# A backbone layer on one core: GLU of three token blocks moved beside the readout, its result kept on chip

## The chip, the core and the metric

The kernel runs on one core of a Trainium2 chip. The metric is the device time of one execution in microseconds, the median of several runs. The engines are PE (TensorE, matmuls), DVE (VectorE), ACT (ScalarE) and POOL (GpSimd); SP (SyncE) issues all loads and stores. Each engine works through its own instructions in order and waits at semaphores for the others. PE's granted clock is given as a share: 1.0 is 2.4 GHz, 0.5 is 1.2 GHz, and a mean between them says how long it ran at which.

## What is computed

One layer over 2048 latent tokens of 1024 channels with a prefix of 256 context tokens. Half of the channels go through RWKV-7 time mixing (a recurrence in both directions), half through a bidirectional S5 state space model; its output y ends in a gated linear unit (GLU):

```python
    z = jax.nn.gelu(y)
    out = z * jax.nn.sigmoid(z @ glu_w.astype(f32) + glu_b.astype(f32))
...
        x = x + mod_x[2] * (jnp.concatenate([rwkv_x, s5_x], axis=-1) @ w_out[layer])
        x = x + mod_x[5] * swiglu(modulate(rmsnorm(x, norm2_g[layer]), mod_x[3], mod_x[4]),
                                  ffn_w1[layer], ffn_w3[layer], ffn_w2[layer])
...
    return rmsnorm(x, final_g)
```

GLU, RWKV readout, output projection and FFN act on each token by itself.

## The kernel before

Tokens are worked through in four blocks of 512, in the tail from block 3 down to block 0, since the backward RWKV direction delivers the last tokens first. All matmuls are float32, written as a high and a low part: `split` (L1140) makes the high part on ACT (L1141) and the low part on DVE (L1142), and a product takes three matmuls, high by high, high by low and low by high.

A scheduler orders the instructions: the code's order is their priority, and an instruction of lower priority goes first where it can start earlier in the scheduler's own timing of the program. On the chip the resulting order of each engine is fixed.

The class `Tail` does what follows the mixers. `glu(b, put)` loads z of a block (L1171; into buffers of the tag s, in the tail ns), splits it, then for each of four groups m of 128 channels: loads and splits 128 columns of weights (wr, wh, wl), loads z again for the gate (L1183, tag t), does 12 matmuls of 512 columns (L1187), tanh (L1189), an affine step (L1190), and the product with z on POOL (L1192). `put` takes the result: `keep` splits it into the tiles H and L, from which the output projection reads; `store` writes it to the DRAM scratch `cat`, and `load` fetches it from there and then keeps it. `readout(b, put)` does the same for the RWKV half, in 8 steps of 128 channels by 256 tokens (first matmul L1207 or L1211, sums L1252, transposition L1257). `outproj` and the second part of `ffn` are one function, `product` (L1293 to L1295, 256 columns each); the first part of `ffn` is L1369 with 512 columns. `norm` makes the FFN's input.

Before the tail proper, `hybrid_block` runs block 3's GLU and output projection together with the last 12 units of the backward RWKV direction (`R.unit`, 128 tokens each: a triangular inverse, mostly on POOL, L1012 and L1019 on PE, then the chain of states L1045, L1050, L1059, L1072, L1074; the result YW is stored by L1083). The GLU of blocks 2, 1 and 0 stands there as well, between the steps of block 3's readout, and stores to `cat`. `ffn(3)` follows with lower priority. When the units are done, the pool f2 takes over the memory of the RWKV pool, and `T.aside` gives GLU and readout their buffers there, from which the steps for the next block run beside the FFN of the one before (`early`).

Of the kernel before, what the change touches and what calls it, by code (L numbers as in the profile page):

```python
# ---- part 1: adaLN vectors, norm1, input projection, conv; one block of tokens after the other
# [8 lines left out]
F32 = mybir.dt.float32  # L10
# [12 lines left out]
AHEAD = 3000     # priority of what feeds the tensor engine  # L23
# [12 lines left out]
ORDER4 = [t for t in ORDER if t[0] == "u"] + [t for t in ORDER if t[0] != "u"]       # of the last block  # L36
PLANE = {"r": 0, "k": 1, "kk": 2, "v": 3}       # of rkvk
CONV = {"r": 0, "k": 1, "v": 2}                 # of the conv's channels
# [28 lines left out]
def rsqrt(nc, y, t, x, out=None, spread=lambda a: a):  # L67
    """out = spread(1 / sqrt(x)), x positive: from the halved exponent, three steps of Newton; y, t: scratch"""
    stt = nc.vector.scalar_tensor_tensor
    nc.vector.tensor_scalar(y.bitcast(I32), x.bitcast(I32), -0.5, float(0x5f3759df), op0=OP.mult, op1=OP.add)  # L70
    for i in range(3):
        stt(t, x, -0.5, y, op0=OP.mult, op1=OP.mult)
        nc.vector.tensor_tensor(t, t, y, op=OP.mult)
        if i < 2 or out is None:
            stt(y, t, 1.5, y, op0=OP.add, op1=OP.mult)
        else:
            stt(out, spread(t), 1.5, spread(y), op0=OP.add, op1=OP.mult)
# [6 lines left out]
def mod_group(tc, I, K, S, wt, st, fp, n, tag="f"):  # L84
    """128 columns of the adaLN product; wt(), st(): tiles of 1024 and 256 words, fp: tag f"""
    nc = tc.nc
    sec, part = divmod(n, 8)
    mw = I["mod_w"][0].rearrange("(k p) c -> p k c", p=P)
    pm = fp.tile([P, 512], F32, name=tag, bufs=2 if tag == "pa" else None)
    w = wt().rearrange("p (k c) -> p k c", k=8)  # L90
    for kh in range(2):
        nc.sync.dma_start(w[:, 4 * kh:4 * kh + 4], mw[:, 4 * kh:4 * kh + 4, n * P:(n + 1) * P])
        for kc in range(4):
            nc.tensor.matmul(pm[32 * kc:32 * kc + 32, 0:P], K["scp"][:, 4 * kh + kc, :], w[:, 4 * kh + kc, :],
                             start=kh == 0, stop=kh == 1)
    st = st()
    rows = st[:, 0:P]
    nc.scalar.activation(rows, pm[:, 0:P], AF.Copy)
    pc = fp.tile([P, 512], F32, name="f")
    if sec in (2, 5):  # L100
        nc.tensor.matmul(pc[0:2, 0:P], K["sel"], rows, start=True, stop=True)
        mb = st[0:1, P:2 * P]
        nc.sync.dma_start(mb, I["mod_b"][:, n * P:(n + 1) * P])
        nc.vector.tensor_add(mb, pc[0:1, 0:P], mb)
        nc.sync.dma_start(S["gate"][sec // 3:sec // 3 + 1, part * P:part * P + P], mb)
    else:
        nc.tensor.matmul(pc[:, 0:2], rows, K["sel"], start=True, stop=True)
        o = VOFF["mod_b"] + n
        nc.vector.tensor_scalar(K["mcol"][:, sec, part, :], pc[:, 0:2], K["vec"][:, o:o + 1], None, op0=OP.add)


def mod_vectors(tc, K, sec, dst, g, j):
    """scale (1 + s) g and shift of one normalisation"""
# [6 lines left out]
class Front:  # L120
    """S: rkvk [4,512,NT], vt [2,NT,512], lora [128,NT], sg [96,NX], u [512,16,144], zh [12,128,3,64], gate [2,1024]"""

    def __init__(self, tc, I, K, S, p, p2, fp):
# [20 lines left out]
        # selectors of one head's row among 8  # L144
# [81 lines left out]
    def conv(self, bi, kind, q, pa):  # L226
        """-> (tile, tokens) with the conv's output for the tokens that this block completes"""
# [31 lines left out]
    def span(self, bi):  # L259
        """tokens that the conv completes with this block"""  # L260
        return ((0, 256), (256, 384), (640, 512), (1152, 512), (1664, 640))[bi]
# [37 lines left out]
    def block(self, bi, aside=iter(()), order=ORDER, wait=0):  # L299
        """aside: work to interleave, one piece after each tile but the first ones (wait)"""  # L300
# [64 lines left out]
# ---- part 2: S5  # L365
# [7 lines left out]
def acc_exp(nc, pool, x, shape, name):  # L373
    """exp(x) to float32's accuracy on DVE; x is overwritten."""
# [90 lines left out]
NTAB = 394      # per pair of groups: L1 68, L2 68, BR 64, BI 64, BS 64, CR 32, CI 32, RHO 2  # L465
# [3 lines left out]
def s5_setup(tc, I, K, S, sp, pp):  # L469
    """Tables of every pair of groups -> S: s5t [16,128,NTAB], s5p [16,128,2,2,144], s5d [64,16,16]"""  # L470
# [33 lines left out]
    # q = (lb - 1) / lam  # L504
# [18 lines left out]
    # mag^16 and phase^16, each twice along the free axis  # L523
# [18 lines left out]
    # to states on partitions: (re, im), then (-im, re)  # L542
# [25 lines left out]
    # B and C  # L568
# [32 lines left out]
    # D on the diagonal of the lag 0 block: rows (g even: 0..15, g odd: 48..63)  # L601
# [14 lines left out]
    # phase tables exp(i phi n), n = 0..143  # L616
# [26 lines left out]
def s5_pair(tc, gp, S, K, DD, g1, g2, ps):  # L643
    """One pair of groups. S: u, s5t, s5p, wd -> z"""
# [39 lines left out]
    # lag blocks  # L684
# [21 lines left out]
    # input -> state  # L706
# [61 lines left out]
def s5_pairs(tc, S, K, DD, gps, sets, ps):  # L768
    """the pairs gps, in the buffers of the sets in turn"""
    for gp in gps:  # L770
        g1, g2 = sets[gp % len(sets)]
        yield from s5_pair(tc, gp, S, K, DD, g1, g2, ps)
        yield


# ---- part 3: RWKV-7 in chunks of 64 tokens, one direction after the other

S05 = math.exp(-0.5)
NU = 18         # units of 128 tokens
# [3 lines left out]
class Rwkv:  # L783
    """S: rkvk, vt, lora -> y [2,512,NX] (per direction), pb [2,512,NX] (r * kd per direction).
    What belongs to the backward direction is reversed within each 128 tokens; only the rows that k and v give to
    BK, BT, AR and V stay in natural order."""

    def __init__(self, tc, I, K, S, pool, pw, ph, nq=2, nb=4):
# [8 lines left out]
        # causal masks; in the backward direction the rows of k and v are in natural order  # L797
        self.MS = r.tile([P, 2, 64], F32, name="MS")        # direction
        self.MI = r.tile([P, 2, 2, 64], F32, name="MI")     # direction, par
# [12 lines left out]
        self.hv = hv = r.tile([P, 8], F32, name="hv")   # ka/2 (4), 1-ka/2 (4)  # L812
# [3 lines left out]
        # low-rank factors in parts, rows (high, high, low) and the bias (high, low) on the inputs' (high, low, high), 1, 1  # L816
        self.W2A = r.tile([98, 2, 512], F32R, name="W2A")
        self.LT = r.tile([98, 2, 256], F32R, name="LT")
        self.back = r.tile([P, 4, 64], F32, name="back")        # the backward direction's state after the context
        nc.vector.tensor_copy(self.LT[96:98], ones[96:98, None, 0:1].to_broadcast([2, 2, 256]))  # L820
        self.SG = r.tile([P, 2, 4, 2, 65], F32, name="SG")      # two units
        nc.gpsimd.memset(self.SG, 0.0)
        self.use(r)
        # unit matrices, lane 8 e + b of 32 holds the columns 4 m + e of matrix b
# [13 lines left out]
    def use(self, pool):  # L838
        """what the units keep, in a pool of its own"""
# [8 lines left out]
    def base(self, h):  # L848
        """first natural token of unit h"""
# [32 lines left out]
    def lora(self, h):  # L882
        """units h and h + 1: tanh of half the low-rank products"""
# [98 lines left out]
    def inverse(self, h, dve):  # L982
# [18 lines left out]
        T2 = r.tile([P, 8, 4, 8], F32, name="T2")     # m, e, b  # L1001
# [94 lines left out]
# ---- part 4: RWKV readout, output projection, FFN, final norm, 512 tokens at a time  # L1096
# [10 lines left out]
class Tail:  # L1107
    """S: y, pb, rkvk (v), sg, z, gate -> out"""
# [18 lines left out]
    def aside(self, f2, fq):  # L1127
        """the parts before the FFN of the next blocks take their buffers here"""
        self.side = (f2, fq, "nt", "ns", "zh", "zl")
        nc = self.nc  # L1130
        self.ER = f2.tile([P, 2, P], F32R, name="ER")       # Cm and blk, both exact
# [12 lines left out]
    def parts(self, b, pool=None):  # L1144
        """the mixer's output as (high, low)"""
# [7 lines left out]
    def store(self, b, k, ts, x):  # L1153
        t0 = 512 * b
        self.nc.sync.dma_start(self.S["cat"][k * P:(k + 1) * P, t0 + ts.start:t0 + ts.stop], x)

    def load(self, b, ks):
        for k in ks:
            x = self.side[0].tile([P, 512], F32, name=self.side[3], bufs=2)
            self.nc.sync.dma_start(x, self.S["cat"][k * P:(k + 1) * P, 512 * b:512 * b + 512])  # L1160
            self.keep(b, k, slice(0, 512), x)

    def glu(self, b, put):
        """z sigmoid(z W + b), z = [channels, token mod 16, token / 16]"""
# [4 lines left out]
        for k in range(4):  # L1169
            z = f2.tile([P, 512], F32, name=tag_s, bufs=2)  # L1170
            nc.sync.dma_start(z.rearrange("p (s j) -> p s j", s=16), zd[k])  # L1171
            zh = f2.tile([P, 512], F32R, name=tag_h, bufs=5)
            zl = f2.tile([P, 512], F32R, name=tag_l, bufs=5)
# [23 lines left out]
    def readout(self, b, put):  # L1197
# [6 lines left out]
        def product(o, w, exact, x, scale=None):  # L1204
            """w^T (scale x), with aside in parts; exact: w has no low part"""
# [18 lines left out]
        for hf in range(2):  # L1224
# [7 lines left out]
            for hp in range(4):  # L1232
# [16 lines left out]
                # the variances with the tokens on the partitions, spread out by the transposition  # L1249
# [21 lines left out]
    def product(self, b, A, n, wsrc, grow, last):  # L1271
        """X1 += gate * (A^T W), A = list of (hi, lo) of [128, 512 tokens], wsrc(k, columns) in DRAM;
        last: with X1 done, its squares are summed up"""
# [107 lines left out]
    def final(self, b):  # L1381
# [8 lines left out]
        for j in range(4):  # L1390
# [8 lines left out]
           "s5t": (16, P, NTAB), "s5p": (16, P, 2, 2, 144), "s5d": (64, 16, 16), "y": (2, 512, NX), "pb": (2, 512, NX),  # L1399
           "cat": (D, NX)}  # L1400
# [7 lines left out]
def hybrid_block(tc, I, out):  # L1408
    with tc.tile_pool(name="dram", bufs=1, space=bass.MemoryType.DRAM) as dp, \
# [50 lines left out]
        with tc.tile_pool(name="f1", bufs=1, side="right") as f1, tc.tile_pool(name="fp", bufs=3, space=PSUM, side="right") as fp:  # L1460
# [5 lines left out]
            rest = chain(*[T.glu(b, T.store) for b in (2, 1, 0)])  # L1466
            for i, _ in enumerate(T.readout(3, T.keep)):
                for _ in range(1 + i % 2):
                    next(rest, None)
            run(rest)  # L1470
# [6 lines left out]
            with tc.tile_pool(name="f2", bufs=1) as f2, tc.tile_pool(name="fq", bufs=3, space=PSUM) as fq:  # L1477
                T.aside(f2, fq)
                for b in (3, 2, 1):
# [3 lines left out]
                    T.load(b - 1, range(4, 8))  # L1483
                    early = T.ffn(b, SPLITS[3:5])
                    for _ in T.readout(b - 1, T.keep):
# [29 lines left out]
```

## Time and profile before

| | |
|---|---|
| median of 3 runs | 3823.46 us (3818.53 to 3835.97) |
| span of the profiled execution, first to last instruction | 3809.6 us |
| median less that span | 13.9 us |
| PE busy | 3423.6 us, 90% |
| mean granted clock | 0.906 |

The span is that of one execution taken by the hardware profiler; the runs' times hold what lies around it as well. "Busy" is the time in which an engine works on an instruction, overlaps counted once in the rows by stretch.

### The profile page before, as it was taken

Reading aid. Unit: us, or ns where it says so; the run is one execution under the profiler, and the core shown is the slowest. Engines: PE = TensorE matmul, PEld = TensorE weight load, DVE = VectorE, ACT = ScalarE, POOL = GpSimd, SP = SyncE. Lnnn points to the kernel's source line nnn. Section 1 sums busy time; section 2 is a strip of 40 time slices with the busy share of each in tenths; the row PEclk is TensorE's granted clock in tenths of the full one; section 3 lists DMA queues with packets and bytes.
Section 4 is the critical chain, followed back from the end, with each engine's and each line's share of the span. In section 5 each row is a group of like instructions: output and inputs, shape, how many; then the busy total and the mean of one; then the engine's idle time right before and its main releaser. Section 6 shows DMA issues by size and latency. Waiting matters only on the chain. (4 is left out here: it accounts for less than half of the span.)

```text
span 3809.6 us, 70313 instructions
## 1 busy us (share of the span) xinstructions
PE 3423.6 (90%) x25311; PEld 2858.0 (75%) x25311; DVE 2480.0 (65%) x4726; ACT 1723.1 (45%) x3785; POOL 1840.0 (48%) x3184
## 2 busy tenths in 40 slices
PE   5698988988777898888889999999999999999998
PEld 3676666666556676677677888988889888998887
DVE  7768777776778978856666647476444854454444
ACT  3565656554434443444455544354333433343333
POOL 3456667567667766766776543223212321231212
PEclk9898989898757876777899999999999999999999
DMA  6654545454233453365623335354333533333333
GB/s 184 195 138 114 150 110 140 131 139 118 76 97 108 136 141 106 95 160 128 147 85 94 97 109 158 106 165 129 103 98 103 173 102 100 106 100 121 103 99 96
DMA packets 789020, 462.34 MB, mean 121 GB/s; under 512 B 182544, under 2 KB 766868, under 8 KB 788672
## 3 DMA queue, kind: packets, MB, share of 16 engines
q1 hardware_dynamic: 788672, 457.85, 42.6%
q8 instruction: 200, 3.28, 0.4%
q14 instruction: 148, 1.21, 0.1%
HBM read 382.34 MB, written 75.36 MB: 120 GB/s over the span
## 5 line engine op out<-in xcount | busy, mean ns | idle before, releaser
L1301 POOL TENSOR_TENSOR X<-X,t 128x256 f32<-128x256 f32 x464 | 380.1, 848 | 940.6 <-DVE t L1298 937.5
L997 POOL TENSOR_TENSOR tmp<-AT,T 128x60 f32<-128x60 f32 (+24 forms) x992 | 402.8, 406 | 252.5 <-DVE AT L990 134.5
L1142 DVE TENSOR_TENSOR wl<-wr,wh 128x512 fp32r<-128x512 f32 x368 | 263.4, 717 | 327.7 <-PE f L1369 280.1
L999 POOL TENSOR_TENSOR T<-T,tmp 128x60 f32<-128x60 f32 (+24 forms) x992 | 423.6, 427 | 64.3
L1141 ACT ACTIVATE wh<-wr 128x512 fp32r<-128x512 f32 x368 | 231.9, 631 | 453.0 <-PE f L1369 394.8
L1142 DVE TENSOR_TENSOR vl<-vr,vh 128x256 fp32r<-128x256 f32 x480 | 256.2, 535 | 265.2 <-ACT vh L1141 264.7
L1294 PE MATMUL f<-vl,gh 128*128 128x256 f32 x1408 | 396.4, 288 | 6.6 <-DVE vl L1142 6.4
L1369 PE MATMUL f<-H,wh 128*128 128x512 f32 x1408 | 389.6, 397 | 9.6 <-ACT s L1372 5.2
L1295 PE MATMUL f<-vh,gl 128*128 128x256 f32 x1408 | 389.4, 284 | 0.0
L1369 PE MATMUL f<-L,wh 128*128 128x512 f32 x1408 | 389.1, 395 | 0.0
L1141 ACT ACTIVATE vh<-vr 128x256 fp32r<-128x256 f32 x480 | 199.3, 416 | 418.4 <-PE f L1295 367.7
L1369 PE MATMUL f<-H,wl 128*128 128x512 f32 x1408 | 385.6, 395 | 1.0 <-DVE wl L1142 1.0
L1293 PE MATMUL f<-vh,gh 128*128 128x256 f32 x1408 | 370.0, 287 | 2.7 <-ACT vh L1141 2.1
L255 DVE SCALAR_TENSOR_TENSOR acc<-zb,cw,acc 128x512 f32<-128x512 f32 (+2 forms) x384 | 314.1, 833 | 46.9 <-ACT acc L251 36.1
L1369 PEld LDWEIGHTS f<-L,wh 128*128 128x128 f32 x1408 | 264.0, 189 | 59.5 <-issue 0.2
L1369 PEld LDWEIGHTS f<-H,wl 128*128 128x128 f32 x1408 | 262.1, 188 | 59.7 <-DVE wl L1142 1.8
L1369 PEld LDWEIGHTS f<-H,wh 128*128 128x128 f32 x1408 | 258.0, 189 | 64.0 <-ACT s L1372 5.8
L1294 PEld LDWEIGHTS f<-vl,gh 128*128 128x128 f32 x1408 | 269.0, 191 | 16.9 <-DVE vl L1142 10.3
L1295 PEld LDWEIGHTS f<-vh,gl 128*128 128x128 f32 x1408 | 269.2, 191 | 1.4
L1293 PEld LDWEIGHTS f<-vh,gh 128*128 128x128 f32 x1408 | 255.4, 191 | 10.8 <-ACT vh L1141 3.6
L222 PE MATMUL pa<-HI,wl 128*128 128x512 f32 (+1 forms) x712 | 210.2, 415 | 49.6 <-POOL wl L219 39.0
L222 PE MATMUL pa<-HI,wh 128*128 128x512 f32 (+1 forms) x712 | 215.7, 424 | 26.6 <-ACT wh L218 14.0
(458 smaller groups left out, 7602.6 us busy)
## 6 DMA issues: line engine op xcount, KB each, us to landing
wr<-in_ffn_w_dram SPq DMA_DIRECT2D x352, 256.0 KB
raw<-in_w_in_dram SPq DMA_DIRECT2D x178, 256.0 KB
vr<-in_ffn_w_dram SPq DMA_DIRECT2D x352, 128.0 KB
ld<-s_rkvk SPq DMA_DIRECT2D x36, 768.0 KB
mraw<-in_mod_w_dram SPq DMA_DIRECT2D x64, 256.0 KB
vr<-in_w_out_dram SPq DMA_DIRECT2D x128, 128.0 KB
gq<-s_gate SPq DMA_DIRECT2D x116, 128.0 KB
SV<-s_vt SPq DMA_DIRECT2D x144, 64.0 KB
```

The costliest lines, as they stand in the source:

```text
L222: nc.tensor.matmul(pa[:, :nt], w[:, kc, :], h[:, 4 * kh + kc, :nt], start=kh + i + kc == 0, stop=kh == 1 and i == 2 and kc == 3)
L255: nc.vector.scalar_tensor_tensor(ag, zb[:, i0 - 1 + a:i0 - 1 + a + nr, e:e + 64], tap(a, e), ag, op0=OP.mult, op1=OP.add)
L997: eng.tensor_tensor(tv, AT[:, l + 1:, l:l + 1].to_broadcast([P, n, m]), T[:, l:l + 1, 0:m].to_broadcast([P, n, m]), op=OP.mult)
L999: eng.tensor_tensor(T[:, l + 1:, 0:m], T[:, l + 1:, 0:m], tv, op=OP.add)
L1141: self.nc.scalar.activation(hi, x, AF.Copy)
L1142: self.nc.vector.tensor_tensor(lo, x, hi.bitcast(F32), op=OP.subtract)
L1293: mm(o, ah[:, js], vh, start=k == 0 and j % 2 == 0, stop=False)
L1294: mm(o, ah[:, js], vl, start=False, stop=False)
L1295: mm(o, al[:, js], vh, start=False, stop=k == n - 1 and j % 2 == 1)
L1301: nc.gpsimd.tensor_tensor(x, x, t[:, j], op=OP.add)
L1369: mm(p, a[:, kc, :], h[:, 4 * kh + kc, :], start=kh + i + kc == 0, stop=kh == 1 and i == 2 and kc == 3)
```

## The change

The GLU of blocks 2, 1 and 0 is no longer worked out during block 3's readout. Each is worked out in the tail, ahead of the readout of the same block in the same interleaving with `early`, and keeps its result in H and L at once. The scratch `cat`, its 12 stores and 12 loads and the functions for them go. The tail's pool f2 gets four buffers each for the parts of z, zh and zl. The text also loses its comments, and its line numbers from 1153 on are 9 to 15 lower.

```diff
-    def store(self, b, k, ts, x):
-        t0 = 512 * b
-        self.nc.sync.dma_start(self.S["cat"][k * P:(k + 1) * P, t0 + ts.start:t0 + ts.stop], x)
-
-    def load(self, b, ks):
-        for k in ks:
-            x = self.side[0].tile([P, 512], F32, name=self.side[3], bufs=2)
-            self.nc.sync.dma_start(x, self.S["cat"][k * P:(k + 1) * P, 512 * b:512 * b + 512])
-            self.keep(b, k, slice(0, 512), x)
-
     def glu(self, b, put):
...
-            zh = f2.tile([P, 512], F32R, name=tag_h, bufs=5)
-            zl = f2.tile([P, 512], F32R, name=tag_l, bufs=5)
+            nb = 5 if f2 is f1 else 4
+            zh = f2.tile([P, 512], F32R, name=tag_h, bufs=nb)
+            zl = f2.tile([P, 512], F32R, name=tag_l, bufs=nb)
...
             T.parts(3)
             run(T.glu(3, T.keep))
             T.outproj(3, range(4, 8))
-            rest = chain(*[T.glu(b, T.store) for b in (2, 1, 0)])
-            for i, _ in enumerate(T.readout(3, T.keep)):
-                for _ in range(1 + i % 2):
-                    next(rest, None)
-            run(rest)
+            run(T.readout(3, T.keep))
             T.outproj(3, range(4))
...
                     T.parts(b - 1, f1 if b == 2 else f2)
-                    T.load(b - 1, range(4, 8))
                     early = T.ffn(b, SPLITS[3:5])
-                    for _ in T.readout(b - 1, T.keep):
+                    for _ in chain(T.glu(b - 1, T.keep), T.readout(b - 1, T.keep)):
                         next(early, None)
                     run(early)
```

On PE, amid the readout of block 3, the order before has GLU matmuls (f<-gh,wh and its kind) between readout (L1207, L1252) and RWKV (L963):

```order
L1187 MATMUL f<-gh,wh 128x512
L1187 MATMUL f<-gl,wh 128x512
L1187 MATMUL f<-gh,wl 128x512
L1207 MATMUL f<-yl,Cm 128x256
L963 MATMUL w<-Q,BK 128x128 x8
L1207 MATMUL f<-pl,RK 128x256
L1207 MATMUL f<-sg,g_17011 128x256
L1252 MATMUL f<-blk,yl 128x2 x2
```

The changed order at the same place has readout (L1198, L1243, L1248, the former L1207, L1252, L1257) and RWKV alone:

```order
L1243 MATMUL f<-blk,yl 128x2 x2
L963 MATMUL w<-Q,BK 128x128 x4
L1198 MATMUL f<-pl,RK 128x256
L963 MATMUL w<-Q,BK 128x128 x4
L1198 MATMUL f<-sg,g_17010 128x256
L1198 MATMUL f<-yl,Cm 128x256
L976 MATMUL w<-ident,BK 128x64 x4
L1248 MATMUL f<-ident,yl 128x128 x2
```

The twelve GLU matmuls on either side of such a step are gone, and the RWKV unit's own (L963, L976) stand next to the readout's.

At the end of the last RWKV unit PE's order before is this, L1293 to L1295 being FFN:

```order
L1074 MATMUL p_22747<-Q,SV 64x64
L1074 MATMUL p_22748<-Q,SV 64x64
L1295 MATMUL f<-vh,gl 128x256
L1293 MATMUL f<-vh,gh 128x256
L1294 MATMUL f<-vl_24651,gh 128x256
```

The changed order there, where L1178 is the GLU (the former L1187) of block 2 and L1360 the FFN (the former L1369):

```order
L1050 MATMUL p_22351<-R,TW_1084 64x64
L1072 MATMUL p_22350<-AR,UV 64x64 x4
L1074 MATMUL p_22350<-Q,SV 64x64 x4
L1072 MATMUL p_22351<-AR,UV 64x64 x4
L1074 MATMUL p_22351<-Q,SV 64x64 x4
L1178 MATMUL f<-zh,wh 128x512 x2
L1178 MATMUL f<-zl,wh 128x512
L1178 MATMUL f<-zh,wl 128x512
```

The last RWKV matmuls follow each other without FFN between them, and the GLU's 24 matmuls on the first two channel groups follow directly; FFN comes behind those.

On SP, the order before at the same moment, from the last store of y on (L1160 loads from `cat`):

```order
L1083 DMA s_y<-YW 128x4x128
L1285 DMA vr<-in_ffn_w_dram 128x256
L1160 DMA ns<-s_cat 128x512
L1285 DMA vr<-in_ffn_w_dram 128x256
L1160 DMA ns<-s_cat 128x512
L1280 DMA gq<-s_gate 128x256
L1326 DMA X_26547<-in_x_dram 128x1024
L1227 DMA sg<-s_sg 96x256
L1326 DMA X_26549<-in_x_dram 128x1024
```

The changed order, where L1161 loads z into the two buffers ns, L1174 loads z for the gate and L1317 loads X:

```order
L1174 DMA t<-s_z 128x16x32
L1354 DMA wr<-in_ffn_w_dram 128x4x128
L1029 DMA UV<-s_vt 64x256 x2
L1083 DMA s_y<-YW 128x4x128
L1161 DMA ns<-s_z 128x16x32 x2
L1317 DMA X_26270<-in_x_dram 128x1024
L1317 DMA X_26272<-in_x_dram 128x1024
L1317 DMA X_26274<-in_x_dram 128x1024
L1218 DMA sg<-s_sg 96x256
L1317 DMA X_26276<-in_x_dram 128x1024
L1228 DMA pl<-s_pb 128x2x256
L1161 DMA ns<-s_z 128x16x32 x2
```

Two of the four z loads of block 2 stand behind the last store of y, and the other two behind four loads of X.

## Rows read from the trace of the kernel before

**Rows 1.** The page's first lines: span, and busy time by engine.

```profile
span 3809.6 us, 70313 instructions
...
PE 3423.6 (90%) x25311; PEld 2858.0 (75%) x25311; DVE 2480.0 (65%) x4726; ACT 1723.1 (45%) x3785; POOL 1840.0 (48%) x3184
```

**Rows 2.** Busy time by stretch: columns as named in the first line.

```profile
core 0: us, PE busy (x) PEld busy (x) DVE busy (x) ACT busy (x) POOL busy (x), PEclk, DMA share, GB/s
...
1760.00:1830.00 70.00, 58.89 (x404) 44.12 (x402) 44.72 (x108) 32.70 (x76) 52.47 (x102) 0.76 0.66 149
1830.00:1872.00 42.00, 37.00 (x328) 28.07 (x330) 31.20 (x70) 24.27 (x58) 29.79 (x59) 0.80 0.65 146
1872.00:1935.00 63.00, 57.88 (x532) 49.33 (x529) 41.93 (x80) 33.80 (x95) 48.75 (x99) 0.95 0.46 127
...
2247.00:2272.00 25.00, 25.00 (x336) 23.18 (x334) 10.33 (x22) 9.48 (x24) 5.95 (x8) 1.00 0.32 98
2272.00:3810.00 1538.00, 1502.15 (x9027) 1329.58 (x9023) 836.26 (x1645) 577.45 (x1273) 380.54 (x471) 0.99 0.39 117
```

**Rows 3.** Line 1160, the loads from cat: issues, and who waited.

```profile
L1160 SPq DMA_DIRECT2D ns<-s_cat x12: 320/327/1289, 2275.9 to 2979.5; - x12
...
  ACT H L1141: 9.9, 7
```

**Rows 4.** The GLU's matmuls (line 1187) alone, by stretch: PE, PEld, clock, DMA.

```profile
1691.00:1760.00 69.00, 3.01 (x12) 2.18 (x12) 0.80 0.47 110
1760.00:1830.00 70.00, 26.32 (x72) 17.41 (x72) 0.76 0.66 149
1830.00:1872.00 42.00, 12.24 (x36) 7.50 (x36) 0.80 0.65 146
1872.00:1935.00 63.00, 7.64 (x24) 5.55 (x24) 0.95 0.46 127
```

**Rows 5.** PE's waits, 1644 to 2272: us in total, times, longest.

```profile
PE f L1207 <- ACT s L1189: 4.4, 2, 4.2
```

**Rows 6.** FFN matmuls of 512 columns (line 1369) alone, in the tail.

```profile
2700.00:2800.00 100.00, 67.34 (x284) 52.42 (x282) 1.00 0.34 101
```

**Rows 7.** Timeline of ACT: start, duration, instruction, idle before and releaser.

```profile
1862.08 0.63 ACT L1141 ACTIVATE gh<-s 128x512 fp32r<-128x512 f32 x1 [0.99 <-DMA s<-s_z]
```

**Rows 8.** Busy time by stretch in the tail, columns as in rows 2.

```profile
2300.00:2350.00 50.00, 48.16 (x282) 42.13 (x282) 36.32 (x106) 24.02 (x53) 13.23 (x17) 1.00 0.49 140
2350.00:2400.00 50.00, 49.21 (x271) 42.39 (x270) 33.85 (x71) 20.08 (x42) 17.30 (x22) 1.00 0.48 140
...
2550.00:2600.00 50.00, 45.98 (x294) 40.89 (x294) 37.08 (x97) 22.69 (x52) 17.66 (x23) 1.00 0.62 190
...
2700.00:2750.00 50.00, 50.00 (x308) 44.68 (x307) 22.83 (x38) 15.93 (x31) 9.62 (x12) 1.00 0.33 100
...
3000.00:3050.00 50.00, 45.87 (x291) 41.16 (x290) 35.56 (x94) 22.05 (x50) 18.13 (x22) 0.97 0.61 188
```

**Rows 9.** Timeline of PE, last unit: its first matmuls of the inverse.

```profile
2249.56 1.94 PE L1012 MATMUL p<-tmp,AY 32*32 32x32 f32 x32
```

**Rows 10.** Timeline of all engines where the last unit ends.

```profile
2268.26 0.78 ACT L1052 ACTIVATE UV<-p 64x256 f32<-64x256 f32 x2 [0.19 <-PE p L1050]
...
2271.73 0.68 PE L1074 MATMUL p<-Q,SV 64*64 64x64 f32 x16
...
2273.24 0.38 SPq L1083 DMA_DIRECT2D s_y<-YW  x1
...
2275.92 0.33 SPq L1160 DMA_DIRECT2D ns<-s_cat  x1
...
2279.15 0.63 ACT L1141 ACTIVATE H<-ns 128x512 fp32r<-128x512 f32 x1 [0.94 <-DMA ns<-s_cat]
```

**Rows 11.** Timeline of DVE: the two steps of a unit's state.

```profile
1805.82 0.87 DVE L1066 TENSOR_TENSOR SV<-c,SV 64x256 f32<-64x256 f32 x2
1806.72 0.87 DVE L1068 TENSOR_TENSOR SV<-SV,EC 64x256 f32<-64x256 f32 x2
```

**Rows 12.** Timeline of SP: issue of the z load that rows 7 split.

```profile
1858.39 0.52 SPq L1171 DMA_DIRECT2D s<-s_z  x1
```

More of the change, by code (lines that the diff above doesn't have):

```diff
@@ L1398 @@
            "zh": (12, P, 3, 64), "gate": (2, D), "wd": (32, 16, 496), "z": (512, 16, P),
-           "s5t": (16, P, NTAB), "s5p": (16, P, 2, 2, 144), "s5d": (64, 16, 16), "y": (2, 512, NX), "pb": (2, 512, NX),
-           "cat": (D, NX)}
+           "s5t": (16, P, NTAB), "s5p": (16, P, 2, 2, 144), "s5d": (64, 16, 16), "y": (2, 512, NX), "pb": (2, 512, NX)}
 def run(steps):
```

## The prediction

> **What bounds the kernel now.** I read the page's engine shares first, then the busy time by stretch, then the waits. TensorE (PE) is busy for 90% of the span [rows 1], and the stretches show two regimes [rows 2]. From the last RWKV unit on (2272 to 3810 us) PE is busy 1502.15 of 1538 us at a granted clock of 0.99: whatever is added there on PE comes out at the end, unless it fills one of the few holes. Before it, from 1760 to 1935 us, PE works on RWKV units, the readout of block 3 and the GLU of blocks 2, 1 and 0, is busy 153.8 of 175 us, and the granted clock is 0.76, 0.80 and 0.95, so it runs a part of that time at 1.2 instead of 2.4 GHz. This is the stretch that the change empties, and the tail is the one that it fills.
>
> **What it removes.** First the round trip: 12 stores and 12 loads of 256 KB. Who waits for them? Only ScalarE, 9.9 us in 7 times, for the loads [rows 3]. PE does not appear there, and each issue costs SyncE 0.33 us. I count this at nothing: what hides it is FFN work on PE (1538 us with 36 us of holes). Without that cover it would be 9.9 us. The four splits of a block into H and L stay; only their input changes.
>
> Second, 144 GLU matmuls leave the RWKV stretch. One row per stretch gives their busy time there: 3.01 + 26.32 + 12.24 + 7.64 = 49.2 us, that is 0.34 us for one [rows 4]. PE runs in order and is the busy engine here, so I take all of it: **-49.2**. The bounds: nothing, if units and readout wait for their own chain as soon as PE has less to do (VectorE and GpSimd, 44.72 and 52.47 of 70 us, are not full); and 65, if the 16 us in which PE idles between 1760 and 1872 (70 - 58.89 and 42 - 37.00) go too. PE waited 4.4 us of these for the GLU's own tanh, which holds a PSUM bank [rows 5]; I set that against chains that are laid bare with less filling, and take nothing for the two.
>
> **What it adds in the tail.** The same 144 matmuls at full clock. 512 columns of FFN take 67.34 us for 284, 0.237 each [rows 6]: **+34.1**. ScalarE and VectorE get some 12 instructions each a block, of about 0.63 us as the split in [rows 7], so 8 us, among FFN work that leaves them idle for 34 and 27 of 50 us (2700:2750, [rows 8]); hidden there, 8 us a block if not. The FFN that fills the RWKV stretch does not change in amount: the built order has 48 matmuls of 512 columns and 61 of 256 more ahead of the last RWKV matmul, and as many fewer behind it (at 0.237 and half of that 18.6 us, moved, not saved).
>
> **The hand-over from RWKV to the tail** is where it loses. Before, FFN matmuls stand between and behind those of the last unit; now that FFN is used up, and the order shows inverse, chain and GLU directly behind each other. Two prices follow.
>
> (a) The bare chain. From the first L1012 (2249.56, [rows 9]) to the end of the last L1074 (2271.73 + 0.68, [rows 10]) lie 22.9 us, filled by FFN (PE 25.00 of 25 us in that stretch, [rows 2]). PE's own part of it is about 9.7 us in ten groups of RWKV matmuls, of which these two are the first and the last. Between them stand five ScalarE copies of up to 0.78 us (the second L1052, [rows 10]) and two pairs on VectorE of 0.87 us [rows 11]: some 14 to 15 us if nothing else is issued. So about **+5** of idle PE (bounds 0, if units on the chip fall behind the order, and 13, the whole chain without PE's part, were nothing overlapped).
>
> (b) The first z. The pool f2 takes over memory of the RWKV pool, so its first load waits for the landing of the last store of y. Before, that load was issued 3.5 us after the last RWKV matmul (2275.92 against 2272.41, [rows 10]) and its split began 3.2 us later. A z load, issued at 1858.39 [rows 12] and split from 1862.08 on [rows 7], took 3.7 us. Now GLU of block 2 waits for that: 3.5 + 3.7 + 0.6 for the split = 7.8 us with nothing to do, then 1.4 us of matmuls on the first two z; loads three and four wait for the two ns buffers, hence for those splits, and take another 3.7 + 0.6 + about 1. PE is through with its 24 matmuls (5.7 us) some 16 us after the last RWKV matmul: **+10.5** idle. Bounds: 4, if store and z land sooner, and 20, if loads three and four queue behind four loads of X.
>
> After such holes the clock is likely to fall. The stretches above show 0.76 to 0.80 where PE idles a ninth to a sixth of the time [rows 2]. Half rate for half of those 24 matmuls is **+3** (0 to 6).
>
> **Blocks 1 and 0.** Their z loads stand in SyncE's order right after norm's, some 90 loads ahead of the first of the GLU's weights, so nothing waits at the start. The readout comes after the GLU there, so it leaves the stretch in which norm, final and X loads meet. PE idled 4.0 and 4.1 us of 50 there (2550:2600, 3000:3050), and 1.8 and 0.8 where readout 2 runs beside FFN alone (2300:2400, [rows 8]). I take **-3** for both (0 to -8).
>
> Sum: -49.2 + 34.1 + 5 + 10.5 + 3 - 3 = +0.4. The profiled execution's span is 3809.6 us; it becomes 3810. The runs' median of 3823.46 is 13.9 above that span, for what lies around it and the spread of runs; I keep that: **3824 us**.
>
> **A rule against row.** The loads of z are pieces of 128 bytes, those of cat whole rows of 2 KB, both 256 KB: 3.7 us from issue to split against 3.2 [rows 7, 10, 12]. The Trainium skill (DMA: Bandwidth & Descriptors, Specifications) says that full rate wants transfers of 512 bytes and more, and speaks so against z loads on the critical path. If by that a z load took four times the 3.2 us, two of them in turn would cost the hand-over 18 us more and the time were 3842. The trace does not bear that out.
>
> **The rivals.**
> *Faster:* the emptied stretch gives back its 16 us of PE idling too, and the chip is late enough against the order that the hand-over loses 4 instead of 10.5: 3810 - 16 - 6.5 = 3787.5, with 13.9: 3801 us. For it: readout and GLU share PSUM banks and buffers there (the 4.4 us). Against: chains of the units remain. Chance 0.23.
>
> *Slower, by z at every block:* the third and fourth t<-s_z of a block wait in SyncE's queue for GpSimd to free a t buffer, FFN weights queue behind them, and PE stalls at blocks 1 and 0 as at block 2: 2 x 10.5 = 21 more, 3845 us. For it: one queue issues all loads, and the t buffers are shared with the products. Against: three weight buffers ahead, and PE in the tail is hardly idle. It decides from 9.5 us a block on. Chance 0.10.
>
> *Slower, by the clock:* with less filling the stretch from 1760 to 1872 falls to the lower clock altogether. PE work left there is 95.9 - 38.6 = 57.3 us at 0.78; at 0.5 it takes 89, so +32: 3856 us. It decides from a mean of 0.58 on. Against: the units before the tail, without FFN, ran on and off at both levels. The Trainium skill (TensorE: Matmul & The Clock Gate, Part 1: The HAM clock gate) says the same of the direction: an engine that is not kept busy is set to half rate. Chance 0.07.
>
> *It does nothing:* it takes out a round trip that nobody waits for, and the moved work costs what it cost. That is a part of my forecast's outcome, not apart from it.
>
> **How the numbers follow.** The forecast, within 0.5% (3804 to 3843 us; about what a measurement of this kernel tells from no change): 0.60, its own range 3809 to 3838. Faster 0.23, slower 0.17. For 8 in 10 the range reaches to the rivals' middles: 3798 to 3849.
>
> **What would show it.** The last RWKV matmul ends near 2272 - 49 + 18.6 + 5 = 2247 us. Directly behind it PE idles some 8 us until a z lands, and PE's busy share in the following 20 us is under 0.7. GLU matmuls in the tail come to 34 to 37 us over the three blocks. PE at norm of blocks 1 and 0 idles less than 4 us in 50. I am wrong if the RWKV stretch ends at 2270 (its chains were the limit) or before 2235 (idling went too), or if PE idles over 8 us a block around the GLU of blocks 1 and 0.

## The result, and the profile after

The changed kernel takes 3844.74 us (median of 5 runs, 3839.87 to 3851.05) against 3818.53 us before on the same chip: ratio 1.0072, 95% interval 1.0051 to 1.0093. It is some 27 us slower. The forecast was no change (3824 us, range 3798 to 3849), and slower stood at 0.17.

The page's first lines of the changed kernel, against [rows 1]:

```profile
span 3841.3 us, 70287 instructions
...
PE 3455.2 (90%) x25311; PEld 2887.4 (75%) x25311; DVE 2485.0 (65%) x4726; ACT 1716.0 (45%) x3779; POOL 1828.1 (48%) x3184
```

PE has the same 25311 matmuls and is busy 31.6 us longer. The change adds no work to PE, so the same matmuls have become slower; 8.8 of the 31.6 us lie ahead of 1690 us, where nothing was changed, and belong to the spread between two executions. Busy time by stretch of the changed kernel says where the rest lies (columns as in [rows 2]). The first row holds four RWKV units, the second the units behind them, the third is the last unit alone, the fourth the tail, and the last two are the norm of blocks 1 and 0:

```profile
1693.70:1918.90 225.20, 203.63 (x1643) 171.26 (x1643) 149.43 (x326) 107.33 (x279) 159.75 (x344) 0.72 0.33 90
1918.90:2270.40 351.50, 331.18 (x3057) 277.92 (x3056) 200.38 (x339) 171.23 (x383) 201.81 (x459) 0.96 0.34 96
2222.30:2270.40 48.10, 43.00 (x402) 38.65 (x400) 18.98 (x36) 14.94 (x34) 28.26 (x66) 0.93 0.36 94
2270.40:3841.30 1570.90, 1521.68 (x9048) 1341.11 (x9048) 855.43 (x1665) 593.20 (x1296) 390.68 (x475) 0.99 0.41 117
...
2520.00:2570.00 50.00, 45.93 (x217) 37.04 (x216) 34.80 (x60) 22.27 (x55) 11.98 (x12) 1.00 0.70 203
2980.00:3030.00 50.00, 45.44 (x219) 37.40 (x218) 35.36 (x62) 22.72 (x58) 11.98 (x12) 0.97 0.68 200
```

The 64 norm matmuls (L1336) in the first of these rows, alone:

```profile
1693.70:1918.90 225.20, 10.36 (x64) 9.59 (x64) 0.72 0.33 90
```

And the same four units, then the rest up to the last RWKV matmul, in the kernel before:

```profile
1690.70:1934.70 244.00, 212.86 (x1725) 172.42 (x1726) 163.14 (x336) 120.95 (x297) 178.32 (x347) 0.83 0.55 132
1934.70:2272.40 337.70, 319.04 (x3012) 269.19 (x3012) 198.75 (x348) 178.97 (x393) 199.48 (x461) 0.96 0.32 93
```

Both kernels come to this stretch at about the same time (1690.7 and 1693.7 us). The forecast had it shorter by 25.6 us (-49.2 of GLU, +18.6 of FFN moved ahead, +5); it is shorter by 5.0 (581.7 against 576.7). The tail is longer by 33.7 (1537.2 against 1570.9). With the 3.0 at the start that is the 31.7 between the spans.

The first four units hold the puzzle. 49.2 us of GLU have left them [rows 4], PE's idle time fell too (31.1 to 21.6 us), 10.4 us of block 3's norm (64 matmuls of L1336) moved in from the unit behind, and still they took only 18.8 us less. Without GLU and norm the work of PE is the same there before and after, but PE is busy with it 193.2 us (203.63 - 10.4) instead of 163.6 (212.86 - 49.22). The clock says why: 0.72 instead of 0.83, and in finer stretches of the changed kernel

```profile
1770.00:1806.00 36.00, 31.86 (x206) 23.63 (x204) 23.59 (x63) 17.23 (x42) 25.61 (x63) 0.50 0.25 63
...
1810.00:1854.00 44.00, 42.31 (x307) 34.95 (x307) 28.16 (x75) 19.32 (x50) 25.38 (x61) 0.50 0.31 81
```

80 us stand at half rate, but for 4 us between them. The two numbers of the second row belong side by side: PE counts as busy for 0.96 of the time, at a clock of 0.50. Busy time at half rate is not work done at full rate.

### The profile page after: what moved, and what is told of

It reads as the page before. It is cut to its first block, busy times and chain, and to the rows that moved or that the text cites. A ratio compares the mean times of both kernels' runs of the same rounds, so it can differ in the third digit from the quotient of the medians.

```text
span 3841.3 us, 70287 instructions
## 1 busy us (share of the span) xinstructions
PE 3455.2 (90%) x25311; PEld 2887.4 (75%) x25311; DVE 2485.0 (65%) x4726; ACT 1716.0 (45%) x3779; POOL 1828.1 (48%) x3184
## 5 line engine op out<-in xcount | busy, mean ns | idle before, releaser
L999 POOL TENSOR_TENSOR T<-T,tmp 128x60 f32<-128x60 f32 (+24 forms) x992 | 414.8, 419 | 64.0
L1142 DVE TENSOR_TENSOR vl<-vr,vh 128x256 fp32r<-128x256 f32 x480 | 265.5, 555 | 243.2 <-ACT vh L1141 242.3
L1360 PE MATMUL f<-H,wh 128*128 128x512 f32 x1408 | 390.1, 398 | 7.1 <-ACT wh L1141 6.0
L1360 PE MATMUL f<-L,wh 128*128 128x512 f32 x1408 | 389.6, 395 | 0.0
L1360 PE MATMUL f<-H,wl 128*128 128x512 f32 x1408 | 387.7, 395 | 1.0 <-DVE wl L1142 1.0
L1360 PEld LDWEIGHTS f<-L,wh 128*128 128x128 f32 x1408 | 263.9, 189 | 59.6
L1360 PEld LDWEIGHTS f<-H,wl 128*128 128x128 f32 x1408 | 262.5, 189 | 59.7 <-DVE wl L1142 1.4
L1360 PEld LDWEIGHTS f<-H,wh 128*128 128x128 f32 x1408 | 257.9, 189 | 62.3 <-ACT wh L1141 8.2
```

The lines of the kernel that those rows point to most:

```text
L999: eng.tensor_tensor(T[:, l + 1:, 0:m], T[:, l + 1:, 0:m], tv, op=OP.add)
L1142: self.nc.vector.tensor_tensor(lo, x, hi.bitcast(F32), op=OP.subtract)
L1360: mm(p, a[:, kc, :], h[:, 4 * kh + kc, :], start=kh + i + kc == 0, stop=kh == 1 and i == 2 and kc == 3)
```

## The experiments

**1. Is it the clock, and is the room free?** If the emptied stretch is slow for want of matmuls, matmuls put back there without anything else of the GLU should cost nothing. `e1_filler` is the changed kernel with 144 matmuls of 512 columns amid block 3's readout, on tiles that lie there (parts of H and L as weights and as data); their results are not used.

```diff
+    def filler(self, b):
+        CH, CL, _ = self.C[b]
+        for n in range(12):
+            pg = self.ftile()
...
+                    self.nc.tensor.matmul(pg, w[:, 4 + n % 4, P * k:P * k + P], h[:, 4 + k, :], ...)
+            yield
...
-            run(T.readout(3, T.keep))
+            rest = T.filler(3)
+            for i, _ in enumerate(T.readout(3, T.keep)):
+                for _ in range(1 + i % 2):
+                    next(rest, None)
+            run(rest)
```

> The changed kernel with 144 matmuls of 512 columns put back into the readout of block 3, on tiles that are there anyway; nobody reads their result, and no load, split or tanh belongs to them. Theory C (the emptied stretch fell to the lower clock, and GLU had been filling that kept it up): the units with the readout take as long as without the filling, within 12 us, the mean clock of the two units around 1760 to 1870 goes from 0.61 and 0.65 back to 0.75 or more, the time is 3844 to 3856 us. Rival A (a matmul costs its own time there, and the 20 us that the prediction misses in that stretch are a new wait of units or readout): 34 to 49 us on top, 3878 to 3893 us, with the clock as low as before or the wait still there.

Measured: 3858.26 us, ratio to before 1.0093 (1.0072 to 1.0115). The same two stretches in that kernel, then the filler (L1159) alone in the first:

```profile
1705.70:1925.30 219.60, 202.72 (x1723) 166.98 (x1723) 141.37 (x314) 102.44 (x270) 150.17 (x323) 0.86 0.32 89
1925.30:2280.70 355.40, 337.27 (x3120) 285.62 (x3120) 212.13 (x351) 176.35 (x390) 211.09 (x477) 0.96 0.34 95
...
1705.70:1925.30 219.60, 42.62 (x144) 30.93 (x144) 0.86 0.32 89
```

The four units are back at a clock of 0.86, and PE's time for all else in them is 160 us (202.72 - 42.62; the norm is not in it), as before the change (163.6). The units themselves take no longer. In four profiled executions with the same instructions there and no filler (the changed kernel, `e7_four_z_buffers`, `e8_two_ffn_steps` and `e2_ffn_first`, all below) they took 218.9 to 225.2 us at clocks of 0.72 to 0.76, with the filler 219.6. Up to the last RWKV matmul, where both kernels have done the same other work, it is 575.0 us with the filler and 576.7 without. So it is the clock that took the gain: 42.6 us of matmuls cost nothing in this place, and as little is to be had by taking them away. The whole kernel is nevertheless slower than the changed one, by 13.5 us in the medians and 8 by the ratios; its theory C had expected 3856 us at most. In the profiled execution, the slowest of its six, the tail is 15 us longer (1585.9) with the same number of matmuls but one, 9 of it idle time, and the four units start 12 us later; why is open.

**2. What was the GLU's price at its old place?** `e3_no_glu` is the kernel before without the GLU of blocks 2, 1 and 0; the loads that fetched its result fetch as many bytes of z. All of that GLU's work is left out.

```diff
-            rest = chain(*[T.glu(b, T.store) for b in (2, 1, 0)])
-            for i, _ in enumerate(T.readout(3, T.keep)):
-                for _ in range(1 + i % 2):
-                    next(rest, None)
-            run(rest)
+            run(T.readout(3, T.keep))
```

> The kernel before without the GLU of blocks 2, 1 and 0: that work is left out, and the tail loads as many bytes of z in its place. What it saves against the kernel before is the price of that GLU at its old place. Theory C: 20 to 30 us, since the clock falls with the filling, 3790 to 3800 us. Rival A (the 49.2 us of the prediction): 45 to 55 us, 3765 to 3775 us.

Measured: 3789.26 us, ratio 0.9911 (0.9889 to 0.9932): some 34 us, not the 49.2 of the rows of its matmuls. Its first four units, the rest up to the last RWKV matmul, and the tail:

```profile
1697.20:1915.60 218.40, 196.98 (x1643) 165.29 (x1643) 148.42 (x326) 107.42 (x279) 160.46 (x344) 0.74 0.34 91
1915.60:2288.80 373.20, 357.54 (x3199) 298.08 (x3198) 210.94 (x354) 181.38 (x399) 203.06 (x460) 0.97 0.34 97
...
2288.80:3787.50 1498.70, 1457.80 (x8763) 1291.03 (x8763) 805.09 (x1614) 560.08 (x1244) 376.10 (x463) 0.99 0.40 117
```

The clock is low as in the changed kernel (0.74 and 0.72), and PE takes 197 us for the same 1643 matmuls that take 204 there. This run splits the result in two: taking the GLU away is worth 34 us (0.0089 of 3822), and putting it into the tail costs 61 (those 34 and the result's 27). The split is not a clean one, since the order moved as well: some 250 more FFN matmuls than before stand ahead of the last RWKV matmul (142 more than in the changed kernel), so the gain shows in a tail that is 38.5 us shorter (1537.2 against 1498.7), not in the stretch, which is 9.9 us longer. How much of the 34 us that order is worth was not tried.

**3. What is that price, if the matmuls are free?** `e5_one_product` keeps everything of the GLU at its old place but two of three matmuls (high by high alone).

```diff
-                for i, (w, h) in enumerate(((wh, 0), (wh, 1), (wl, 0))):
+                ops = ((wh, 0), (wh, 1), (wl, 0))[:3 if b == 3 else 1]
+                for i, (w, h) in enumerate(ops):
```

> The kernel before, with one matmul of three in the GLU of blocks 2, 1 and 0 (high part by high part alone, 48 matmuls instead of 144); the loads of z and weights, the splits, tanh, the products on GpSimd and the round trip through cat all stay. Theory 'companions': the GLU's matmuls are free there, as the 144 that were added to the emptied stretch were, and its price of some 30 us lies in what goes with them, so the time changes by 0 to -8 us against before (ratio 0.998 to 1.000). Rival 'PE work pays': 96 matmuls fewer at 0.237 to 0.34 us are 23 to 33 us less (ratio 0.991 to 0.994).

Measured: 3819.5 us, ratio 1.0002 (0.9984 to 1.0020). 96 matmuls fewer change nothing: from the start of the four units to the last RWKV matmul it is 581.6 us, with all three products 581.7. The four units, the rest, and the 48 GLU matmuls left (L1188), alone:

```profile
1702.30:1934.80 232.50, 192.71 (x1627) 157.12 (x1626) 168.41 (x335) 121.88 (x303) 172.13 (x334) 0.77 0.58 138
1934.80:2283.90 349.10, 332.22 (x3012) 279.94 (x3012) 199.57 (x348) 174.81 (x383) 200.89 (x471) 0.93 0.31 89
...
1702.00:1935.00 233.00, 22.64 (x48) 11.92 (x48) 0.77 0.58 138
```

In the four units the clock gives back only a part. GLU's busy time is 26.6 us less there (49.22 - 22.64); PE is busy 6.4 us longer with all else, at 0.77 instead of 0.83, and idles 8.7 us more, so the units are 11.5 us shorter. Those 11.5 are lost again in the units behind, where the same 3012 matmuls run at 0.93 instead of 0.96; no run shows that this comes from the edit. That the whole time stays is shown by twelve runs; where in the kernel it is given back, by this one profile alone.

So 144 matmuls added to this stretch and 96 removed from it do not make it longer or shorter, and leaving out the whole GLU saves some 34 us. What is left to explain them is what goes with the matmuls (loads, splits, tanh, products, stores), the other order, and the last 48 matmuls, which were not taken out apart from the rest. Four runs looked for one thing among the companions. `e6_one_z_load` multiplies the gate with the high part of z that is on chip, and drops twelve of the z loads; its result is cut to that part.

```diff
-            z = f1.tile([P, 512], F32, name="t", bufs=2)
-            nc.sync.dma_start(z.rearrange("p (s j) -> p s j", s=16), zd[m])
+            if b == 3:
+                z = f1.tile([P, 512], F32, name="t", bufs=2)
+                nc.sync.dma_start(z.rearrange("p (s j) -> p s j", s=16), zd[m])
+            else:
+                z = Z[m][0].bitcast(F32)
```

> The kernel before, with the second load of z left out in the GLU of blocks 2, 1 and 0: the gate multiplies the high part of z, which is on chip, so twelve loads of 256 KB in pieces of 128 bytes go, and the result is that of a z cut to its high part. Theory 'companions', in its form that the DMA engines are the cost: a quarter of the GLU's 48 transfers there (12 weight, 24 z, 12 stores to cat) goes, and 7 to 12 us with it (ratio 0.997 to 0.998). Rival 'GpSimd, splits and buffers are the cost': 0 to -3 us, within what the runs can tell.

Measured: 3829.82 us, ratio 1.0025 (1.0007 to 1.0042), if anything slower. `e9_product_on_dve`:

```diff
-            nc.gpsimd.tensor_tensor(o.rearrange("p (j s) -> p s j", s=16), sg.rearrange("p (s j) -> p s j", s=16),
+            (nc.gpsimd if b == 3 else nc.vector).tensor_tensor(o.rearrange("p (j s) -> p s j", s=16), sg.rearrange("p (s j) -> p s j", s=16),
```

> The kernel before, with the product with z of the GLU of blocks 2, 1 and 0 on VectorE instead of GpSimd; all else stays. Theory 'companions', in its form that GpSimd is the cost (12 products of 1.35 us stand in the queue of the engine that does the triangular inverse, busy 52 of 70 us there): some 16 us less, ratio 0.995 to 0.997. Rival 'the readout's and the units' chains are delayed by every engine's share alike' (ScalarE 23, VectorE 27 and GpSimd 16 us of GLU work in those units): VectorE gets what GpSimd loses, and the time stays within 5 us of before.

Measured: 3817.59 us, ratio 0.9991 (0.9976 to 1.0006). `e10_product_in_place`:

```diff
+            if b < 3:
+                nc.gpsimd.tensor_tensor(sg, sg, z, op=OP.mult)
+                put(b, 4 + m, slice(0, 512), sg)
+                yield
+                continue
             o = f2.tile([P, 512], F32, name=tag_s, bufs=2)
```

> The kernel before, with the product of the GLU of blocks 2, 1 and 0 written in place on GpSimd: it takes no second buffer s, cat holds tokens in z's order, and the split after the round trip puts them right. Theory 'companions', in its form that the two buffers s are the cost (loads of z, tanh and product take turns in them; ScalarE waited 5 to 10 us for them there): 5 to 15 us less than before, ratio 0.996 to 0.999. Rival 'shares of the engines': within 5 us of before.

Measured: 3831.97 us, ratio 1.0034 (1.0017 to 1.0051), slower where a gain was expected. `e11_in_place_on_dve` is this with `nc.vector` in the added product.

> Both edits of the two kernels ahead of it: product on VectorE and in place. If GpSimd and the buffers are the price of the GLU at its old place, the two add up: 15 to 25 us less than before, ratio 0.993 to 0.996, and this is the kernel that beats both. Rival 'shares of the engines': within 5 us of before.

Measured: 3828.87 us, ratio 1.0019 (1.0005 to 1.0032). No half of the z traffic, no engine for the product and no second buffer is the price by itself, and none of these beats the kernel before. Two of them, `e6_one_z_load` and `e10_product_in_place`, also let the scheduler order the units anew (some 270 more matmuls stand ahead of the last RWKV matmul than before), so they test the edit together with another order. Which of the companions costs the 34 us, or whether all do by delaying the chains of readout and units alike, stays open.

**4. The hand-over.** `e7_four_z_buffers` is the changed kernel with the third and fourth z in the buffers nt, so that no load of X stands ahead of them.

```diff
-            z = f2.tile([P, 512], F32, name=tag_s, bufs=2)
+            z = f2.tile([P, 512], F32, name=tag_s if f2 is f1 or k < 2 else self.side[2], bufs=2)
```

> The changed kernel, with the third and fourth z of a block in the tail loaded into the two buffers nt instead of ns, so that all four loads of block 2 are issued directly behind the last store of y and ahead of the loads of X; nothing else is different at the hand-over. Theory 'hand-over': the second idle piece of 5.35 us goes, and GLU of block 2 is through 5 to 8 us sooner; the time is 5 to 8 us under the changed kernel's (ratio to before 1.005 to 1.006). Rival 'given back': what is gained there is lost again in block 2's readout, which meets the same FFN filling sooner: no difference.

Measured: 3845.76 us, ratio 1.0072 (1.0048 to 1.0097). The timeline of the changed kernel around its last RWKV matmul, to compare with [rows 10] (PE, ACT, SP):

```profile
2269.72 0.68 PE L1074 MATMUL p<-Q,SV 64*64 64x64 f32 x8
...
2273.32 2.06 SPq L1161 DMA_DIRECT2D ns<-s_z  x2
2275.44 2.17 SPq L1317 DMA_DIRECT2D X<-in_x_dram  x3
2276.74 0.63 ACT L1141 ACTIVATE zh<-ns 128x512 fp32r<-128x512 f32 x1 [1.40 <-DMA ns<-s_z]
...
2277.47 1.19 PE L1178 MATMUL f<-zh,wh 128*128 128x512 f32 x2 [7.07 <-ACT zh L1141]
...
2279.28 6.18 SPq L1161 DMA_DIRECT2D ns<-s_z  x2
...
2286.71 0.63 ACT L1141 ACTIVATE zh<-ns 128x512 fp32r<-128x512 f32 x1 [2.56 <-DMA ns<-s_z]
...
2287.39 1.22 PE L1178 MATMUL f<-zh,wh 128*128 128x512 f32 x2 [5.35 <-ACT zh L1141]
```

And with all four loads in front:

```profile
2277.50 1.98 SPq L1161 DMA_DIRECT2D ns<-s_z  x2
2279.53 3.10 SPq L1161 DMA_DIRECT2D nt<-s_z  x2
...
2281.66 1.19 PE L1178 MATMUL f<-zh,wh 128*128 128x512 f32 x2 [7.08 <-ACT zh L1141]
...
2284.35 1.05 PE L1178 MATMUL f<-zh,wh 128*128 128x512 f32 x2
```

PE waited twice, 7.07 and 5.35 us; the second wait is gone, and the part from the last RWKV matmul to the norm of block 2 takes 242.9 us instead of 249.5. The edit takes out the buffer and the place behind the X loads at once, so it shows that the wait can be removed, not which of the two made it. In the whole time 6.6 us are less than the two intervals, 8 to 9 us to either side, can tell, and the medians do not show it.

The other side of the hand-over is FFN as filling. `e8_two_ffn_steps` and `e2_ffn_first` put two and four steps of early FFN ahead of block 2's GLU:

```diff
                     early = T.ffn(b, SPLITS[3:5])
+                    if b == 3:
+                        next(early, None)
+                        next(early, None)
```

> The changed kernel, with two steps of early FFN (instead of none, and of the four of the earlier run) ahead of the tail's first GLU: they fill PE during the last unit. Theory 'hand-over': the 5.1 us of idle PE in the last unit and the half clock behind it go, -5 to -9 us, and the idle time for z partly (0 to -6); two steps less beside block 2's readout cost less than half of the +38 us that four cost: 0 to -10 us against the changed kernel. Rival 'moved on': filling is short in the whole stretch from 2250 to 2500 us, and what is taken out of the readout stalls there in full: +5 to +20 us.

> The changed kernel with four steps of early FFN ahead of the GLU of block 2, so that FFN stands between and behind the last RWKV matmuls and z has time to land. If the hand-over costs what the trace shows (5 us of bare chain, 12.4 us of waits for z, 3 to 4 us of half clock): 16 to 21 us less than the changed kernel, 3824 to 3829 us. Rival (the loads of z, X and weights meet in any case and PE waits a little later): within 6 us of the changed kernel, 3839 to 3846 us. Either way the stretch before 2220 us stays as it is, with its clock of 0.61 and 0.65.

Measured: 3859.9 us, ratio 1.0112 (1.0084 to 1.0140), with two steps; 3864.21 us, ratio 1.0108 (1.0083 to 1.0132), with four. Both are slower than the changed kernel: each of their twelve runs took longer than its slowest (3851.05). With four, the last unit and the part to block 2's norm:

```profile
2232.70:2302.20 69.50, 69.50 (x544) 58.99 (x542) 29.23 (x51) 25.11 (x50) 28.27 (x66) 1.00 0.37 103
2302.20:2540.00 237.80, 217.36 (x1319) 194.64 (x1317) 135.26 (x313) 95.13 (x224) 68.90 (x85) 0.91 0.44 119
```

The bare chain is filled without a gap, and 20.4 us of idle time and a clock of 0.91 stand behind it, where readout and output projection of block 2 now have less FFN beside them. Over both parts PE idles as long as in the changed kernel (there 5.1 + 15.9 us); what makes them 9.7 us longer (307.3 against 297.6) is the clock, at which the same matmuls take 10.2 us more. PE's waits behind the chain are spread over many, with four steps

```profile
PE f L1284 <- ACT H L1141: 4.6, 3, 2.6
PE f L1284 <- ACT vh L1141: 4.4, 4, 3.2
PE f L1285 <- DVE vl L1142: 3.2, 4, 2.0
PE f L1202 <- DVE vl L1254: 2.8, 4, 1.4
```

and with two steps the wait for z stands as it was, since it hangs on the last store of y and not on PE (12.4 us in two times, the longest 6.7):

```profile
PE f L1178 <- ACT zh L1141: 12.4, 2, 6.7
```

Filling is a stock: FFN of block 3 covers last unit, z and readout of block 2, and it is short for all three once GLU is no longer part of it.

**5. A part of the change.** `e4_block2_back` leaves the GLU of block 2 at its old place, through cat, and does blocks 1 and 0 in the tail.

```diff
+            rest = T.glu(2, T.store)
...
+                    if b == 3:
+                        T.load(b - 1, range(4, 8))
-                    for _ in chain(T.glu(b - 1, T.keep), T.readout(b - 1, T.keep)):
+                    for _ in chain(T.glu(b - 1, T.keep) if b < 3 else (), T.readout(b - 1, T.keep)):
```

> GLU of block 2 at its old place, through DRAM; blocks 1 and 0 in the tail as changed. The hand-over has no z to wait for, a third of the filling is back. Theory C with the hand-over as seen: 11 us of GLU in the tail and some 20 us at the hand-over go, 3 to 8 us come back in the stretch: 3818 to 3830 us. Rival (the cost sits in blocks 1 and 0, whose GLU makes PE wait in the tail): no more than 8 us gained, 3836 us or above.

Measured: 3823.09 us, ratio 1.0003 (0.9988 to 1.0018): as before. The part from its last RWKV matmul to block 2's norm has 7.7 us of idle time instead of 15.8:

```profile
2289.20:2487.20 198.00, 190.33 (x1264) 173.19 (x1263) 125.08 (x299) 85.24 (x213) 67.06 (x81) 0.98 0.47 134
```

With blocks 1 and 0 moved, the time is that of before; what the whole change loses comes with moving block 2, whose GLU stands at the hand-over itself. No version that ran beats the kernel before.

## Why the prediction was right in its range and wrong in its sum

The measured 3844.74 us lies inside the stated range, near its upper end, which the rivals' middles had set. The sum behind the range gave no change and missed by some 27 us, so the range held by its width and by luck, not by its mechanism.

**The step that failed** is "PE runs in order and is the busy engine here, so I take all of it: -49.2". The rows gave the GLU's busy time, and I took busy time for time that comes back. A third of it did not: 34 us are what leaving it out saves there, and those are not the matmuls' alone, as the runs with 144 added and 96 removed show. I had read the 0.76 and 0.80 of [rows 2] as a cost on the GLU's matmuls (0.34 instead of 0.237 us each), not as a sign that this stretch has PE time to spare.

**The rival that came nearest** is "slower, by the clock": 0.07, priced at +32 if the units from 1760 to 1872 fell to 0.5 altogether, and decisive from a mean of 0.58 on. The two middle units fell to 0.61 and 0.65 (1759 to 1869), so its condition was not quite met, and of the 25.6 us expected of the whole stretch 20.6 are missing. Its mechanism was right, its chance too low: I set the other units, "on and off at both levels", against it, which were no evidence for a stretch that loses 144 long matmuls. The Trainium skill (TensorE: Matmul & The Clock Gate, Part 1: The HAM clock gate), which I had named beside it, says that an engine not kept busy is set to half rate; the trace agrees in direction (0.83 to 0.72).

**My own test** said that I am wrong if the RWKV stretch ends at 2270, and put that down to its chains. It ended at 2270.4, but not for the chains: PE idled less in its first four units than before, not more.

**The tail**, GLU's matmuls first. L1178 alone, in the hand-over and behind it:

```profile
2270.40:2300.00 29.60, 9.32 (x24) 6.74 (x24) 0.77 0.66 167
2300.00:3841.00 1541.00, 30.12 (x120) 22.16 (x120) 1.00 0.40 116
```

39.4 us, where 34.1 + 3 were forecast. The first 24 take 9.3 instead of 5.7 us, +3.6 for the +3. (a) The bare chain idles 5.1 us (48.10 - 43.00), forecast 5. Its clock was not forecast:

```profile
2250.00:2264.00 14.00, 10.28 (x129) 9.02 (x128) 4.52 (x10) 4.46 (x10) 3.53 (x10) 0.76 0.42 78
```

0.76 in 14 us is 6.7 us at half rate, at most 3.4 us lost. (b) z idles 7.07 + 5.35 = 12.4 us, forecast 10.5; the loads were issued 2.9 us behind the last matmul (3.5 forecast), and the second pair stood behind the X loads that the order had shown, 7.4 us from its issue to its split. The bound of 20 with that mechanism was too far, the chosen value a little short. Pieces of 128 bytes cost little: the first z was split 3.4 us after its issue (2273.32 to 2276.74), the one from cat 3.2 [rows 10]. The -3 for blocks 1 and 0 did not come: PE idles 4.1 and 4.6 of 50 us at the norms, as in [rows 8]. Together 2.3 + 1.9 + 3.4 + 3 = 10.6 us over the forecast's 49.6, and the ratios of the runs say about 61. By the profiles the stretch up to the last RWKV matmul missed by 20.6 us, the tail by 7.7 (33.7 where 34.1 + 10.5 + 3 - 3 - 18.6 = 26.0 was forecast), and 3.0 lie ahead of both. The rival that z is late at every block did not happen: PE has no wait for z at blocks 1 and 0. Nor did the faster one: of PE's idle time in the emptied stretch 9.5 us did go, but the clock outweighed them. The round trip through cat was rightly counted at nothing as far as waits go; whether its stores are part of the 34 us was not tried alone.

So -49.2 + 49.6 became about -34 + 61. Both terms missed toward slower, and the first by more.

The 13.9 us that the forecast put around the span were mostly spread: in the changed kernel's profiled execution 1.8 us lie around it (3843.07 less 3841.3). If it was as much before, the profiled execution of before took 3811 us, faster than the median of its runs, and the two profiles lie 31.7 us apart where the ratio of the runs says 27.

## What to carry to other kernels

Before moving matmuls out of a stretch, read its granted clock: where it stands well under 1.0, as here at 0.72 to 0.86, added matmuls can be free and removed ones gain little, since the clock answers to them. Measure what a block of work is worth by leaving it out, not by the sum of its busy rows, and look at whether the order moved with it. Filling at a change of phase is a stock: before taking some away, count what each later wait would need of it, since moving it forward only moves the hole.

## What the runs showed that I had not expected

PE's busy share does not tell its clock: it is 0.96 at a granted 0.50 from 1810 to 1854 us, and 0.92 at 1.00 from 2520 to 2570 us (45.93 of 50). Forty readout matmuls (L1198) of the same shapes took 21.35 us in the changed kernel, and the same forty 15.39 us with the filler beside them:

```profile
1759.00:1868.90 109.90, 21.35 (x40) 9.77 (x40) 0.63 0.32 86
```

```profile
1767.90:1876.80 108.90, 15.39 (x40) 6.97 (x40) 0.83 0.29 78
```

The start of the 22nd RWKV unit, ahead of which nothing was changed, lay between 1689.6 and 1708.9 us over the 13 profiled executions. A difference of some ten us between two profiles is no finding unless both are read from the same event on, and the clock of one execution differs from the next behind that event too: the four units of the changed kernel, in four executions with the same instructions, took 218.9 to 225.2 us.
